# Weight low halves kept on chip between the two streams of a feed-forward up projection, and the inner products of that stage begun three pieces later

## The chip, the cores and the metric

The kernel runs on one core of a Trainium2 chip. The metric is the device time in microseconds (us) of one execution. A core has TensorE (matrix products, with weight loads beside them), VectorE, ScalarE, GpSimd, and SyncE, which here only issues loads. In profile lines they are PE (PEld for weight loads), DVE, ACT, POOL and SP.

## The reference

Two layers run over 256 latent tokens (`x`) and 256 context tokens (`xc`) of width 1024. Each layer has a mixer with three branches and then a convolutional feed-forward part; the change lies in the feed-forward part of the first layer, where both streams go through the same weights:

```python
def conv_ffn(h, w_up, conv_w, conv_b, w_down):
    u = h @ w_up                                  # (256, 1024) @ (1024, 5632)
    up = jnp.pad(u, ((0, 0), (1, 1), (0, 0)))
    u = up[:, :-2] * conv_w[0] + up[:, 1:-1] * conv_w[1] + up[:, 2:] * conv_w[2] + conv_b
    a, g = jnp.split(u, 2, axis=-1)
    return (a * jax.nn.silu(g)) @ w_down
...
    mod = (jax.nn.silu(c) @ w_mod[l] + b_mod[l])[:, None, :]
    mod_c = jax.nn.silu(c_ctx) @ w_mod[l] + b_mod[l]
    sh1, sc1, ga1, sh2, sc2, ga2 = jnp.split(mod, 6, axis=-1)
...
    x = x + ga1 * rms_norm(o, g_post_mix[l])
    f = conv_ffn(modulate(rms_norm(x, g_pre_ffn[l]), sh2, sc2), w_up[l], conv_w[l], conv_b[l], w_down[l])
    x = x + ga2 * rms_norm(f, g_post_ffn[l])
    if not last:
        ...
        xc = xc + cga1 * rms_norm(oc, g_post_mix[l])
        fc = conv_ffn(modulate(rms_norm(xc, g_pre_ffn[l]), csh2, csc2), w_up[l], conv_w[l], conv_b[l], w_down[l])
        xc = xc + cga2 * rms_norm(fc, g_post_ffn[l])
```

## The kernel before

**Split products.** Every float32 matrix is split into a high half (rounded to the matrix format, `hi`) and a low half (`lo`, the float32 value less `hi`). A product is three matrix products: high by high, high by low and low by high (`mm3`). The activations stand split in `HThi` and `HTlo`, 1024 channels by 512 tokens, of which columns 0 to 255 are the context and 256 to 511 the latent tokens.

**Pieces.** The whole kernel is a list `prog` of `Piece`s. A piece takes 512 KB of weights: here two blocks of 128 input channels by 512 output channels. Its weights are loaded to a `raw` buffer (five in all) by SyncE, ScalarE casts the high half (`split_hi`, L201), VectorE subtracts for the low half (`split_lo`, L205), and `emit` issues the products. A piece gives its raw buffer back at the end of `split_lo` (`use`), which lets the next load be issued. `run` goes through the list in order. Before it emits a piece it splits pieces ahead until two pieces that are still to come have been split. Pieces that hold no matrix product (the inner products below) do not count in these two, and are issued on VectorE as soon as the splitting reaches them. Instructions of one engine run in the order in which the program issues them. The tiles `whi` and `wlo` rotate through four buffers each.

**The up projection of the first layer.** `up(blk, (t0, t1))` appends the four pieces of block `blk` (256 value and 256 gate channels) for the tokens t0 to t1. The order is block 0 latent, block 1 latent, block 0 context, block 1 context, and then blocks 2 to 10 for both streams at once. So the weights of blocks 0 and 1 are loaded and split twice, in pieces `f0` to `f0 + 7` and again in `f0 + 8` to `f0 + 15`, because the context activations come later than the latent ones: the chain `c1c` (residual, normalisation, transposes, scaling, split) runs as side work, one step after each piece, and is finished before block 0 context. A 256-token piece is 24 products of 256 columns, a 512-token piece 24 of 512 columns. Two groups of 256 tokens share a PSUM bank. The two-group banks of blocks 0 and 1 and the four banks of block 2 come from the same four buffers, so that block 2 uses again the banks that the last 256-token blocks held. Odd blocks from 3 on use four others.

**Evacuation.** At the end of a block's last piece `ev_up` empties each group: ScalarE applies the middle convolution tap and the bias (L1356), VectorE adds the two neighbour taps (L1359; two large and two single-column instructions a group), later ScalarE applies silu (L1378, issued after the next piece), and GpSimd multiplies value by gate into `hT` (L1379).

**Inner products.** `mod_dot` computes modulation vectors (`ga2` of this layer, `sh1` and `sc1` of the next) on VectorE: for each 128 of 1024 outputs a 512 KB row block is loaded and multiplied with the condition vector of each stream, with accumulation (L451), so two instructions a piece. The 24 pieces are placed among the list's pieces by `spread(first, last, pieces)`, evenly from index `first` to `last`; here `first` is `f0 + 16`, the first piece of block 2.

**Slots.** `u()` hands out one of eight large slots, the longest free first, and `u_free` gives it back. In this stage the residual rows of both streams hold two, and each `hT` tile (four blocks of 128 channels) one, six at the end.

Of the kernel before, what the change touches and what calls it, by code (L numbers as in the profile page):

```python
# [9 lines left out]
F32R = mybir.dt.float32r  # L10
# [21 lines left out]
class Raw:  # L32
    def __init__(self, src, kk, n, early=False):
        self.early = early
        self.src, self.kk, self.n, self.tile, self.left = src, kk, n, None, 0


class Piece:
    def __init__(self, raw, emit, k0=0, kn=0, split=True, pre=None, side=1, need=None, share=None, dot=False):
        self.raw, self.emit, self.k0, self.kn, self.split = raw, emit, k0, kn, split  # L40
        self.pre, self.side, self.need = pre, side, need
        self.hi = self.lo = None
        self.dot = dot
        self.hold = self.fence = False
        self.share = share
        if raw:
            raw.left += 1


class Builder:  # L50
# [115 lines left out]
    def run(self):  # L166
        nc = self.nc
        prog = self.prog
        raws = []
        for p in prog:  # L170
            if p.raw and (not raws or raws[-1] is not p.raw):
                raws.append(p.raw)
        state = {"raw": 0, "live": 0, "split": 0}
        RB = 5

        def dma():
            while state["raw"] < len(raws):
                r = raws[state["raw"]]
                if r.early and self.free:
                    r.tile = self.u([128, r.kk, r.n], name="raw")  # L180
                elif state["live"] < RB:
                    r.early = False
                    r.tile = self.p_raw.tile([128, r.kk, r.n], F32, tag="raw", name="raw")
                    state["live"] += 1
                else:
                    break
                nc.sync.dma_start(out=r.tile, in_=r.src)
                state["raw"] += 1

        def use(p):  # L190
            p.raw.left -= 1
            if p.raw.left == 0:
                if p.raw.early:
                    self.u_free(p.raw.tile)
                else:
                    state["live"] -= 1
                dma()

        def split_hi(p):
            p.hi = self.p_w.tile([128, p.kn, p.raw.n], F32R, tag="hi", name="whi")  # L200
            nc.scalar.copy(p.hi, p.raw.tile[:, p.k0:p.k0 + p.kn, :])  # L201

        def split_lo(p):
            p.lo = self.p_w.tile([128, p.kn, p.raw.n], F32R, tag="lo", name="wlo")
            nc.vector.tensor_tensor(p.lo, p.raw.tile[:, p.k0:p.k0 + p.kn, :], p.hi.bitcast(F32), op=ALU.subtract)  # L205
            use(p)

        def split(p):
            if p.split:
                if p.hi is None:  # L210
                    split_hi(p)
                split_lo(p)

        def next_hi():
            q = prog[state["split"]]
            split_hi(q)
            return lambda: split_lo(q)
        self.next_hi = next_hi

        dma()  # L220
        ahead = 0
        for i, p in enumerate(prog):
            if i and prog[i].split and state["split"] > i:
                ahead -= 1
            if p.hold:
                p.need()
                if p.share:
                    state["split"] = i + 1
                split(prog[state["split"]])
                if state["split"] > i:  # L230
                    ahead += 1
                state["split"] += 1
                p.then()
            while state["split"] < len(prog) and state["split"] <= i + 6:
                q = prog[state["split"]]
                if q.hold and state["split"] > i or q.lo is None and state["split"] > i and prog[state["split"] - 1].fence:
                    break
                if state["split"] > i and q.split:
                    if ahead == 2:
                        break  # L240
                    ahead += 1
                if q.pre:
                    q.pre()
                if q.lo is None:
                    split(q)
                if q.dot:
                    q.emit(q.raw.tile)
                    use(q)
                state["split"] += 1
            if p.need and not p.hold:  # L250
                p.need()
            later, self.later = self.later, []
            if p.share:
                p.emit(p.share.hi, p.share.lo)
            elif p.split:
                p.emit(p.hi, p.lo)
            elif not p.dot:
                p.emit(p.raw.tile)
                use(p)
            for f in later:  # L260
                f()
            for _ in range(p.side):
                self.step()
# [851 lines left out]
    def layer(self, l):  # L1115
# [229 lines left out]
        def ev_up(blk):  # L1345
            def f(g, b):
                j, t0, t1 = g
                a = 2 * blk + j % 2
                ch = a if j < 2 else NFT + a
                n = t1 - t0  # L1350
                ta = self.t((128, n), name="ta")
                if L0:
                    tv, bv = self.halves(ta), self.unwoven(b[:, :n])
                else:
                    tv, bv = ta.unsqueeze(1), b[:, :n].unsqueeze(1)
                nc.scalar.activation(out=tv, in_=bv, func=ACTF.Identity, scale=cw[:, ch, 1:2], bias=cw[:, ch, 3:4])  # L1356

                def tap(o, x, t):
                    nc.vector.scalar_tensor_tensor(o, x, cw[:, ch, t:t + 1], o, op0=ALU.mult, op1=ALU.add)  # L1359

                def taps():
                    w = tv.shape[2]
                    tap(tv[:, :, 1:w], bv[:, :, 0:w - 1], 0)
                    tap(tv[:, :, 0:w - 1], bv[:, :, 1:w], 2)
                    if w == 128:
                        tap(tv[:, 1, 0:1], bv[:, 0, w - 1:w], 0)
                        tap(tv[:, 0, w - 1:w], bv[:, 1, 0:1], 2)
                    if j < 2:
                        st["ta", a] = ta
                        return  # L1370
                    if (l, "h", a // 4) not in st:
                        st[l, "h", a // 4] = self.u([128, 4, T], name="hT")
                    off = t0 - lat_all[0]
                    av = st.pop(("ta", a))
                    hv = st[l, "h", a // 4][:, a % 4, off:off + n]

                    def gate():
                        nc.scalar.activation(out=ta, in_=ta, func=ACTF.Silu)  # L1378
                        nc.gpsimd.tensor_tensor(hv, av, ta, op=ALU.mult)  # L1379
                    self.later.append(gate)  # L1380
                return taps
            return f
# [3 lines left out]
        def up(blk, r, **kw):  # L1386
            self.block(wu[:, :, blk, :], 8, 512, "wst", g4(r), X, ev_up(blk), main=4 if blk % 2 == 0 or (L0 and blk < 2) else 0,
                       pair=L0, **kw)
        f0 = len(self.prog)
        if L0:  # L1390
            up(0, (256, 512), need=lambda: self.finish("c1l"))
            up(1, (256, 512))
            up(0, (0, 256), need=lambda: self.finish("c1c"))
            up(1, (0, 256))
            for blk in range(2, 11):
                up(blk, (0, 512))
            self.spread(f0 + 16, len(self.prog), [p for l1, k in ((0, "ga2"), (1, "sh1"), (1, "sc1")) for p in self.mod_dot(l1, k)])
        else:
            for blk in range(11):
                up(blk, (256, 512))  # L1400
# [199 lines left out]
```

## Time and profile before

| | |
|---|---|
| median of 3 runs | 1506.92 us (1506.75 to 1507.0) |
| profiled execution | 1506.16 us, of which span 1504.4 us |
| granted TensorE clock, mean | 0.988 |
| TensorE, VectorE, ScalarE, GpSimd busy | 1442.5, 1073.0, 730.8, 212.4 us |
| low halves (L205) | 330 instructions, 413.3 us |
| inner products (L451) | 128 instructions, 157.4 us |
| first up projection of the first layer | about 580 to 826 us of the span |

The busy times are shares of one span and overlap. Products are pipelined: each is listed with its whole length, but the next begins before it ends. So the rate is read from the distance of the starts. In a timeline line stand the start, the length, the engine, the source line, the operation, the tiles written and read, the shape, the number of merged instructions, and in brackets the idle time before and what ended it. In a line of waits stand who waited for whom, the total, the count and the longest. In a table by windows stand, for each stretch, its length, and the busy time of each engine with its instruction count, the granted clock, the share of the DMA engines and GB/s. In the chain, a line is a start, a length and what ran.

### The profile page before, as it was taken

The numbers are of one execution on the slowest core, as the hardware profiler recorded it, in microseconds if no ns is written. First come the engines' busy times: TensorE is split into PE (matmuls) and PEld (weight loads), VectorE is DVE, ScalarE is ACT, GpSimd is POOL, SyncE is SP. The second block draws the span as 40 slices with busy tenths as digits, with TensorE's granted clock in tenths as the row PEclk, the third lists the DMA queues.
The fourth block names the chain that finished last, engine by engine and source line by source line (L and its number), as shares of the span: only waits on it lengthen the run. The fifth ranks groups of instructions, "written<-read, shape, count | busy, mean of one in ns | idle before, by whom it ended". The sixth has DMA issues, their size and how long they took to land.

```text
span 1504.4 us, 22921 instructions
## 1 busy us (share of the span) xinstructions
PE 1442.5 (96%) x8681; PEld 1251.2 (83%) x8681; DVE 1073.0 (71%) x1872; ACT 730.8 (49%) x1343; POOL 212.4 (14%) x312
## 2 busy tenths in 40 slices
PE   6999998999999999799999999999999899899997
PEld 3877786778888889788888888887978789799986
DVE  4438788776846578988887787738896556778874
ACT  3434443443455357433444566535544355566663
POOL 2000021002520121111111010100200330312100
PEclk9999999999999999999999999999999999999999
DMA  9623333333642356555454777634454545455662
GB/s 336 199 78 121 102 127 98 90 102 104 175 134 78 98 183 195 182 182 170 146 178 136 236 234 247 222 120 125 141 166 143 192 96 169 154 182 184 209 207 88
DMA packets 103806, 238.07 MB, mean 158 GB/s; under 512 B 8416, under 2 KB 18720, under 8 KB 103568
## 3 DMA queue, kind: packets, MB, share of 16 engines
q1 hardware_dynamic: 99472, 224.56, 46.8%
q0 software_dynamic: 4224, 12.05, 3.0%
q8 instruction: 68, 1.11, 0.3%
q14 instruction: 42, 0.34, 0.1%
HBM read 235.50 MB, written 1.08 MB: 157 GB/s over the span
## 4 chain that ended last, share of the span: by engine, by line
PE 82%; DVE 8%; ACT 3%; issue 3%; POOL 2%; DMA 1%; SPq 0%; DVEq 0%; POOLq 0%; ACTq 0%
PE bank L319 68%; PE bank L703 3%; PE bank L717 3%; PE bank L667 2%; PE bank L1028 2%; DVE wlo L205 2%; DVE ta L1359 1%; DVE jnk L451 1%; PE bank L421 1%; PE bank L664 1%; ACT whi L201 1%; PE bank L1005 1%; DMA raw<-in_w_mod 1%; DMA mb<-mrow 1%; POOL t L819 1%
## 5 line engine op out<-in xcount | busy, mean ns | idle before, releaser
L205 DVE TENSOR_TENSOR wlo<-raw,whi 128x1024 fp32r<-128x1024 f32 (+1 forms) x330 | 413.3, 1265 | 162.3 <-ACT whi L201 160.8
L319 PE MATMUL bank<-HThi,whi 128*128 128x256 f32 (+1 forms) x1408 | 464.5, 330 | 8.8 <-DVE ta L1359 4.5
L319 PE MATMUL bank<-HThi,wlo 128*128 128x256 f32 (+1 forms) x1408 | 459.9, 327 | 7.2 <-DVE wlo L205 7.0
L319 PE MATMUL bank<-HTlo,whi 128*128 128x256 f32 (+1 forms) x1408 | 459.6, 326 | 0.5 <-DVE HTlo L586 0.5
L201 ACT CAST whi<-raw 128x1024 fp32r<-128x1024 f32 (+1 forms) x330 | 335.8, 1037 | 175.1 <-PE bank L319 126.4
L319 PEld LDWEIGHTS bank<-HThi,whi 128*128 128x128 f32 x1408 | 270.2, 192 | 40.4 <-issue 15.5
L319 PEld LDWEIGHTS bank<-HThi,wlo 128*128 128x128 f32 x1408 | 270.2, 192 | 26.8 <-DVE wlo L205 8.7
L319 PEld LDWEIGHTS bank<-HTlo,whi 128*128 128x128 f32 x1408 | 270.5, 192 | 18.7 <-DVE HTlo L586 1.2
L319 PE MATMUL bank<-whi,xs 128*128 128x512 f32 x528 | 159.9, 381 | 0.9 <-DVE ta L1359 0.8
L451 DVE SCALAR_TENSOR_TENSOR jnk<-raw,CB 128x1024 bf16<-128x1024 f32 x128 | 157.4, 1229 | 1.8
L319 PE MATMUL bank<-whi,HThi 128*128 128x512 f32 (+1 forms) x384 | 142.5, 371 | 0.0
L1359 DVE SCALAR_TENSOR_TENSOR ta<-bank,cw,ta 128x255 f32<-128x255 f32 (+2 forms) x224 | 110.7, 527 | 41.7 <-ACT ta L1356 37.6
L319 PE MATMUL bank<-wlo,HThi 128*128 128x512 f32 (+1 forms) x384 | 139.1, 362 | 0.0
L319 PE MATMUL bank<-whi,HTlo 128*128 128x512 f32 (+1 forms) x384 | 139.1, 362 | 0.0
L319 PEld LDWEIGHTS bank<-whi,xs 128*128 128x128 f32 x528 | 99.8, 189 | 16.6 <-ACT ta L1378 1.3
L1356 ACT ACTIVATE ta<-bank,cw 128x256 f32<-128x256 f32 (+1 forms) x96 | 61.2, 646 | 101.9 <-PE bank L319 100.2
L679 ACT ACTIVATE pr<-bank,mn 128x512 f32<-128x512 f32 (+1 forms) x96 | 58.5, 614 | 89.0 <-DVE mn L676 80.6
L1379 POOL TENSOR_TENSOR hT<-ta 128x256 f32<-128x256 f32 (+1 forms) x48 | 56.6, 1182 | 309.3 <-ACT ta L1378 309.0
L319 PE MATMUL bank<-wlo,xs 128*128 128x512 f32 x264 | 100.1, 379 | 0.0
L319 PEld LDWEIGHTS bank<-whi,HThi 128*128 128x128 f32 x384 | 72.6, 189 | 20.4 <-issue 10.9
L319 PEld LDWEIGHTS bank<-whi,HTlo 128*128 128x128 f32 x384 | 72.6, 189 | 8.6
L319 PEld LDWEIGHTS bank<-wlo,HThi 128*128 128x128 f32 x384 | 72.6, 189 | 8.0
(228 smaller groups left out, 1728.9 us busy)
## 6 DMA issues: line engine op xcount, KB each, us to landing
raw<-in_w_in SPq DMA_DIRECT2D x112, 512.0 KB, 3.9
raw<-in_w_up SPq DMA_DIRECT2D x96, 512.0 KB, 4.6
raw<-in_w_modT SPq DMA_DIRECT2D x80, 512.0 KB, 4.2
raw<-in_w_down SPq DMA_DIRECT2D x66, 512.0 KB, 4.6
raw<-in_w_branch SPq DMA_DIRECT2D x24, 512.0 KB, 4.0
raw<-in_w_out SPq DMA_DIRECT2D x24, 512.0 KB, 4.2
raw<-in_w_mod SPq DMA_DIRECT2D x16, 512.0 KB, 10.5
nab<-in_nabias POOLq DMA_DIRECT2D x16, 256.0 KB, 4.1
```

The lines of the kernel that those rows point to most:

```text
L201: nc.scalar.copy(p.hi, p.raw.tile[:, p.k0:p.k0 + p.kn, :])
L205: nc.vector.tensor_tensor(p.lo, p.raw.tile[:, p.k0:p.k0 + p.kn, :], p.hi.bitcast(F32), op=ALU.subtract)
L319: nc.tensor.matmul(out, l, self.woven(r), start=first and i == 0, stop=last and i == 2)
L451: nc.vector.scalar_tensor_tensor(self.jnk, rt[:, 0, :], 1.0, self.CB[:, s, :], op0=ALU.mult, op1=ALU.mult, accum_out=dst[:, j, s:s + 1])
L667: nc.tensor.matmul(b, q[:, c0:c0 + 128], k[:, 0:512], start=True, stop=True)
L679: nc.scalar.activation(out=pt[:, w * i:w * i + w], in_=b[:, w * i:w * i + w], func=ACTF.Exp, scale=-1.0, bias=mn[:, i:i + 1], accum_out=mn ...
L703: nc.tensor.transpose(b[:, o:o + 128], pt[:, 128 * i:128 * i + 128], self.I)
L717: nc.tensor.matmul(b[64 * par:64 * par + 64, 0:w], v_of(p, par, kt), pTs[par][:, w * kt:w * kt + w], start=kt == 0, stop=kt == nkt - 1)
L1028: nc.tensor.matmul(b[:, d, 0:129], v[:, o:o + 128], V[:, s, h, :], start=n == 0, stop=n == len(sl) - 1)
L1356: nc.scalar.activation(out=tv, in_=bv, func=ACTF.Identity, scale=cw[:, ch, 1:2], bias=cw[:, ch, 3:4])
L1359: nc.vector.scalar_tensor_tensor(o, x, cw[:, ch, t:t + 1], o, op0=ALU.mult, op1=ALU.add)
L1379: nc.gpsimd.tensor_tensor(hv, av, ta, op=ALU.mult)
```

## The change

The low halves of pieces `f0` to `f0 + 7` are written to slots from `u()`, two pieces to a slot, four slots in all. Pieces `f0 + 8` to `f0 + 15` take these tiles as their low half and leave the subtraction out; they still load their weights and cast their high half. After the second piece of a pair has been emitted for the context, the slot is given back. The 24 inner-product pieces are spread from `f0 + 19` instead of `f0 + 16`.

```diff
         def split_lo(p):
-            p.lo = self.p_w.tile([128, p.kn, p.raw.n], F32R, tag="lo", name="wlo")
+            if p.lo_of:
+                p.lo = p.lo_of.lo
+                use(p)
+                return
+            p.lo = p.lo_at() if p.lo_at else self.p_w.tile([128, p.kn, p.raw.n], F32R, tag="lo", name="wlo")
             nc.vector.tensor_tensor(p.lo, p.raw.tile[:, p.k0:p.k0 + p.kn, :], p.hi.bitcast(F32), op=ALU.subtract)
             use(p)
...
             up(1, (256, 512))
             up(0, (0, 256), need=lambda: self.finish("c1c"))
             up(1, (0, 256))
+
+            kept = {}
+            for k in range(8):
+                p, q = self.prog[f0 + k], self.prog[f0 + 8 + k]
+
+                def put(k=k):
+                    if k % 2 == 0:
+                        kept[k // 2] = self.u([128, 2, 2, 512], F32R, name="keep")
+                    return kept[k // 2][:, k % 2]
+
+                def done(hi, lo, k=k, emit=q.emit):
+                    emit(hi, lo)
+                    if k % 2:
+                        self.u_free(kept[k // 2])
+                p.lo_at, q.lo_of, q.emit = put, p, done
             for blk in range(2, 11):
                 up(blk, (0, 512))
-            self.spread(f0 + 16, len(self.prog), [p for l1, k in ((0, "ga2"), (1, "sh1"), (1, "sc1")) for p in self.mod_dot(l1, k)])
+            self.spread(f0 + 19, len(self.prog), [p for l1, k in ((0, "ga2"), (1, "sh1"), (1, "sc1")) for p in self.mod_dot(l1, k)])
```

More of the change, by code (lines that the diff above doesn't have):

```diff
@@ L42, in __init__ @@
         self.hi = self.lo = None
+        self.lo_at = self.lo_of = None
         self.dot = dot
```

## Prediction

> **What bounds the kernel now.** I read the page first (shares, then the chain that ended last), then TensorE's waits in the stage that is edited, then the order of time on TensorE, VectorE and ScalarE there, and last the stretch behind it.
>
> ```profile
> PE 1442.5 (96%) x8681; PEld 1251.2 (83%) x8681; DVE 1073.0 (71%) x1872; ACT 730.8 (49%) x1343; POOL 212.4 (14%) x312
> ...
> PE 82%; DVE 8%; ACT 3%; issue 3%; POOL 2%; DMA 1%; SPq 0%; DVEq 0%; POOLq 0%; ACTq 0%
> ...
> PE bank L319 <- DVE wlo L205: 4.6, 4, 1.8
> PE bank L319 <- DVE ta L1359: 4.5, 2, 3.5
> ...
> core 0: us, PE busy (x) PEld busy (x) DVE busy (x) ACT busy (x) POOL busy (x), PEclk, DMA share, GB/s
> 604.77:639.39 34.62, 27.10 (x218) 25.41 (x216) 31.37 (x67) 15.33 (x26) 4.49 (x5) 1.00 0.59 194
> 640.00:660.70 20.70, 20.70 (x98) 18.12 (x97) 18.90 (x25) 9.55 (x12) 2.45 (x3) 1.00 0.56 178
> 764.30:785.00 20.70, 20.70 (x98) 18.12 (x97) 19.05 (x25) 9.08 (x12) 2.57 (x3) 1.00 0.54 178
> ...
> 639.84 166.19 PE bank L319 x770
> ```
>
> Over the whole span TensorE is busy 96% and carries 82% of the chain: only places where it stands still can give time. The waits are those of 602 to 640 us: six, four on the subtraction that makes a low half (L205), two on the convolution taps (L1359). In the third group, 604.77 to 639.39 is the context half of blocks 0 and 1: VectorE is busy 31.37 of 34.62 us, TensorE 27.10, so VectorE sets the pace. Behind it the chain is one piece, 770 products in 166.19 us (0.2158 us each): TensorE never waits there, so what the earlier stage gains is passed on whole.
>
> I number the weight pieces of the up projection 0 to 15: 0-3 and 4-7 are blocks 0 and 1 for the latent rows, 8-11 and 12-15 the same for the context rows; piece 16 is the first of block 2. A piece is 24 products.
>
> ```profile
> 602.78 0.38 PE L319 MATMUL bank<-HThi,wlo 128*128 128x256 f32 x1 [1.57 <-DVE wlo L205]
> 603.00 0.28 PE L319 MATMUL bank<-HThi,whi 128*128 128x256 f32 x1
> ...
> 603.89 0.28 PE L319 MATMUL bank<-HThi,wlo 128*128 128x256 f32 x1
> ...
> 606.05 0.38 PE L319 MATMUL bank<-HThi,wlo 128*128 128x256 f32 x1 [0.32 <-DVE wlo L205]
> 613.46 0.38 PE L319 MATMUL bank<-HThi,wlo 128*128 128x256 f32 x1 [1.78 <-DVE wlo L205]
> 625.37 0.38 PE L319 MATMUL bank<-HThi,wlo 128*128 128x256 f32 x1 [0.92 <-DVE wlo L205]
> 636.81 0.45 PE L319 MATMUL bank<-HThi,whi 128*128 128x512 f32 x1 [3.46 <-DVE ta L1359]
> 639.39 0.45 PE L319 MATMUL bank<-HThi,whi 128*128 128x512 f32 x1 [1.04 <-DVE ta L1359]
> ```
>
> From 603.00 to 603.89 are eight steps of 0.111 us, so an unhindered piece takes 24 x 0.11125 = 2.67 us. The waits end at the third product of pieces 7, 8, 10 and 14 (the first that needs a low half), and at groups 2 and 3 of piece 16, whose PSUM banks the taps of piece 15 must have read. From 602.78 to 639.39 (36.61 us) TensorE does 22 + 8 x 24 = 214 short products (23.81 us) and 18 long ones (3.88 us): 8.9 us are lost. Split by the same count (24, 48, 96, then 46 + 12 long, then 6 long products between the rows) this is 0.6 before piece 8, 2.1 before piece 10, 1.2 before piece 14, 3.7 and 1.3 at piece 16.
>
> **The change part by part.** The order on VectorE is that of the program:
>
> ```profile
> 604.16 0.69 DVE L586 TENSOR_TENSOR HTlo<-ht,HThi 128x512 fp32r<-128x512 f32 x1
> 604.77 2.35 DVE L205 TENSOR_TENSOR wlo<-raw,whi 128x1024 fp32r<-128x1024 f32 x2
> 607.04 5.22 DVE L1359 SCALAR_TENSOR_TENSOR ta<-bank,cw,ta 128x254 f32<-128x254 f32 x16
> 612.19 1.21 DVE L205 TENSOR_TENSOR wlo<-raw,whi 128x1024 fp32r<-128x1024 f32 x1
> 613.75 3.60 DVE L205 TENSOR_TENSOR wlo<-raw,whi 128x1024 fp32r<-128x1024 f32 x3 [0.35 <-ACT whi L201]
> 618.73 5.45 DVE L1359 SCALAR_TENSOR_TENSOR ta<-bank,cw,ta 128x254 f32<-128x254 f32 x16 [1.37 <-ACT ta L1356]
> 624.09 1.22 DVE L205 TENSOR_TENSOR wlo<-raw,whi 128x1024 fp32r<-128x1024 f32 x1
> 625.65 1.34 DVE L205 TENSOR_TENSOR wlo<-raw,whi 128x1024 fp32r<-128x1024 f32 x1 [0.34 <-ACT whi L201]
> 626.92 1.21 DVE L451 SCALAR_TENSOR_TENSOR jnk<-raw,CB 128x1024 bf16<-128x1024 f32 x1
> ...
> 629.33 2.36 DVE L205 TENSOR_TENSOR wlo<-raw,whi 128x1024 fp32r<-128x1024 f32 x2
> ...
> 634.01 5.23 DVE L1359 SCALAR_TENSOR_TENSOR ta<-bank,cw,ta 128x254 f32<-128x254 f32 x16
> ```
>
> Behind the last low half of the context activations (L586) these are the low halves of pieces 8, 9; taps of 7; low halves of 10; 11, 12, 13; taps of 11; low halves of 14 and 15; a first inner-product piece (two passes over a row of 1024, one per stream, 626.92 to 629.33, 2.4 us); low halves of 16, 17; a second inner-product piece (to 634.01); taps of 15. The change takes out the eight subtractions of pieces 8 to 15 (some 1.2 us each) and puts both inner-product pieces behind the taps of 15, since the first now stands in front of piece 19 and the loop prepares only two pieces ahead.
>
> The casts of the high halves stay. ScalarE's rows give the two delays that the new order keeps:
>
> ```profile
> 604.23 1.06 ACT L1356 ACTIVATE ta<-bank,cw 128x256 f32<-128x256 f32 x2
> 612.68 2.93 ACT L201 CAST whi<-raw 128x1024 fp32r<-128x1024 f32 x3
> 617.62 1.02 ACT L1356 ACTIVATE ta<-bank,cw 128x256 f32<-128x256 f32 x2 [2.00 <-PE bank L319]
> 624.59 2.93 ACT L201 CAST whi<-raw 128x1024 fp32r<-128x1024 f32 x3
> 629.47 1.02 ACT L1356 ACTIVATE ta<-bank,cw 128x256 f32<-128x256 f32 x2 [1.95 <-PE bank L319]
> ```
>
> Taps start 1.11 us after ScalarE's first evacuation where VectorE is free (617.62 to 618.73). ScalarE starts 0.3 to 0.4 us after the twelfth product of a block's last piece (617.62 against 613.46 + 34 x 0.11125 = 617.24; 629.47 against 629.15). Three casts follow 5.86 us after a start of taps (618.73 to 624.59), behind the gates of that block.
>
> The new course, from 602.78, up to which nothing changes:
> - Piece 8 starts 22 products later, at 605.23, and has its low half. The last write of its context activations (604.16, 0.69 us) ends by 604.9, in time.
> - Taps of 7 start at 604.23 + 1.11 = 605.34 instead of 607.04; casts of 11 to 13 at about 611.0 instead of 612.68, done for 11 by 612.0, and piece 11 begins at 605.23 + 3 x 2.67 = 613.24.
> - Taps of 11: twelfth product 614.58, ScalarE 614.95, VectorE 616.06. Casts of 15, 16, 17 at 621.9 to 624.9; piece 15 begins at 623.92, its cast is done at 622.9. Low halves of 16 and 17 end by 626.25.
> - Taps of 15: twelfth product 625.26, ScalarE 625.57, VectorE 626.68. In the old run group 2 of piece 16 started 2.80 us and group 3 5.38 us after these taps began (634.01 to 636.81 and 639.39). So group 2 may start at 629.48 where TensorE is ready at 626.59 + 12 x 0.2158 = 629.18 (0.3 lost), and group 3 at 632.06 where it is ready at 630.78 (1.3 lost).
>
> Group 3 of piece 16 then starts at 632.06 instead of 639.39: **7.3 us less** (8.9 lost before, 1.6 left). What is late next is the chain from the last product of piece 15 through ScalarE and the taps to the bank. In parts: with the products left where they are, they would push the taps of 15 to about 628.6 and the gain would be 5.4; with the products moved alone, ScalarE's 629.47 would let the taps start at 630.6 and the gain would be 3.4.
>
> Parts that I cost at nothing, and their bounds:
> - The moved products (24 pieces over 33 body pieces instead of 36) fall into the stretch where TensorE never waits. A block there takes 20.7 us; blocks with three of them now keep VectorE busy 18.90 and 19.05, and 24 over 33 is 2.9 per block. Cover 1.6 us a block. Without cover the two early ones would cost 2 x 2.4 = 4.8.
> - Low halves of 0 to 7 go to another buffer with the same shape, by the same instruction: 0 by the row of 1.22, up to 0.1 each by the slowest row (1.34), of which only piece 7's lies on the path.
> - SyncE's loads keep their number. A raw buffer of pieces 8 to 15 is given back by ScalarE's cast instead of the subtraction, so loads go out earlier; each inner-product load goes out three pieces later, behind the loads of 16 to 18, and is needed only by VectorE. Piece 17's load goes out after cast 12 (612.9) and lands 4.5 us later by the row below, against its cast at 623.9. A piece in 2.67 us asks 196 GB/s; the stage already moved 194 with the DMA engines 0.59 busy.
> - Four slots are held for the kept halves, beside two of residual rows and one of gated outputs: seven of eight. The context rows' load gets another slot, whose last readers, the merged branch products, ended by 541 (L1204 below, last start 539.3); the load stays where it is, at 565.14.
>
> ```profile
> raw<-in_w_up SPq DMA_DIRECT2D x25, 512.0 KB, 4.5
> ...
> 658.82 3.56 POOL L1379 TENSOR_TENSOR hT<-ta 128x512 f32<-128x512 f32 x2 [18.25 <-ACT ta L1378]
> ...
> 659.19 4.27 DVE L205 TENSOR_TENSOR wlo<-raw,whi 128x1024 fp32r<-128x1024 f32 x2
> ...
> L1204 DVE SCALAR_TENSOR_TENSOR HTlo<-sig,HThi x8: 677/680/1766, 526.0 to 539.3; 128x512 fp32r<-128x512 f32 x8
> ...
> 565.14 0.79 POOL L642 DMA_DIRECT2D x<-in_ctx  x1
> ...
> 598.84 0.97 DVE L585 CAST HThi<-ht 128x512 fp32r<-128x512 f32 x1 [0.62 <-ACT ht L582]
> ...
> 598.00 0.36 PE L319 MATMUL bank<-HThi,whi 128*128 128x256 f32 x1
> ```
>
> **The rivals.**
> 1. Slower: VectorE becomes the bound of blocks 2 to 10. Beside GpSimd's two gated products (658.82) a pair of subtractions took 4.27 us where the pair of 629.33 took 2.36: 1.9 us. Inner products also read two operands, and more of them now follow each block's taps. Three a block come to 4 x 1.2 + 3 x 2.4 + 5.9 = 17.9 us without such a loss; two losses make 21.7, 1.0 over the 20.7, and eight blocks would give 8.0 back: 1507.6. It decides from 3.7 us of loss a block. Against it: the blocks that have three read 18.90 and 19.05, losses included, with TensorE unbroken.
> [...]
> 2. Pieces share a kept tile in pairs. If products waited for the whole tile, piece 6 would wait for the low half of 7 (its third product at 602.78 instead of some 598.3; one piece, 2.67 us, lost) and piece 2 some 1.1 us for that of 3: gain 3.5, 1503.4. Against it: at 598.84 VectorE writes the context half of HThi while TensorE, from 598.00, reads the latent half with no wait, so halves of a tile are kept apart.
> 3. The change does half of what it says: the products still come up ahead of the taps of 15. Gain 5.4: 1501.5. Against it: the order above is just what the two-piece look-ahead gives.
>
> **How the numbers follow.** The profiled execution took 1506.16 us (span 1504.4, 1.8 around it), 0.8 below the median of the runs, 1506.92; the difference is taken from the median: 1506.92 - 7.3 = 1499.6. Chances: the forecast 0.80 (its own range 1498.6 to 1500.6, VectorE ready for the taps of 15 0.4 us early, or 1 us late); rival 2 0.06; rival 3 0.04; rival 1 0.07, of which 0.04 at the full price or more and 0.03 where it eats most of the gain; 0.03 for a gain of 8 to 9 (all 8.9 us). A measurement of this kernel tells about 0.2% (3.0 us) from no change. Faster: 0.80 + 0.06 + 0.04 + 0.03, less 0.02 for rival 2 with a small gain, 0.91; same 0.05; slower 0.04. The range runs from 1498.0 (all of 8.9) to 1502.0 (rival 3, and the bound of the slower subtractions).
>
> **What would show it.** Right: ten subtractions between 604.77 and the second block's start become two; no wait on L205 in pieces 8 to 15; taps of 7, 11 and 15 start near 605.3, 616.1 and 626.7; the first inner-product pass after the taps of 15; one or two short waits on L1359 at piece 16, together 1.6 us; then one unbroken piece of some 166 us or more on TensorE. Wrong: a wait on L205 in pieces 2, 4 or 6 (rival 2), an inner product ahead of the taps of 15 (rival 3), waits on L1359 or L205 between 640 and 800 (rival 1), or the casts of the high halves becoming what pieces 11 or 15 wait for.

## The result, and the profile after

The changed kernel takes 1498.34 us in the median (1495.86 to 1500.67), against 1506.96 before (1506.75 to 1507.04): ratio 0.9941, 95% interval 0.9929 to 0.9953, so 7.1 to 10.7 us less. Forecast were 1499.6 in a range of 1498.0 to 1502.0. The profiled execution took 1497.82 us, its span 1496.0 against 1504.4.

The lines of the file have moved by five: the subtraction is L210, the products L324, the taps L1364, the inner products L456. First TensorE's waits from 605 to 640 us, then windows of the stage and of two blocks behind it (columns as before), then the long piece of the chain:

```profile
PE bank L324 <- DVE ta L1364: 1.0, 1, 1.0
...
605.06:632.37 27.31, 26.27 (x218) 25.18 (x216) 17.46 (x52) 16.27 (x27) 3.71 (x5) 1.00 0.62 207
633.00:653.70 20.70, 20.70 (x98) 18.12 (x97) 18.60 (x25) 8.70 (x11) 2.86 (x3) 1.00 0.53 178
715.80:736.50 20.70, 20.70 (x98) 18.12 (x97) 17.75 (x24) 8.24 (x11) 2.56 (x3) 1.00 0.55 178
...
632.37 178.96 PE bank L324 x828
```

Of the five waits in pieces 8 to 16 one is left, the last, at a bank of piece 16. VectorE is busy 17.46 of 27.31 us where it was 31.37 of 34.62: it no longer sets the pace, and TensorE is busy 26.27. Behind the stage the chain is one piece again. VectorE's order of time in the new stage, and TensorE's starts of piece 0, of piece 7 behind its wait, and of groups 0, 2 and 3 of piece 16:

```profile
605.62 5.25 DVE L1364 SCALAR_TENSOR_TENSOR ta<-bank,cw,ta 128x254 f32<-128x254 f32 x16 [0.47 <-ACT ta L1361]
616.38 5.24 DVE L1364 SCALAR_TENSOR_TENSOR ta<-bank,cw,ta 128x254 f32<-128x254 f32 x16 [5.52 <-ACT ta L1361]
624.05 2.36 DVE L210 TENSOR_TENSOR wlo<-raw,whi 128x1024 fp32r<-128x1024 f32 x2 [2.43 <-ACT whi L202]
626.99 5.24 DVE L1364 SCALAR_TENSOR_TENSOR ta<-bank,cw,ta 128x254 f32<-128x254 f32 x16 [0.57 <-ACT ta L1361]
632.14 1.21 DVE L210 TENSOR_TENSOR wlo<-raw,whi 128x1024 fp32r<-128x1024 f32 x1
633.27 1.77 DVE L456 SCALAR_TENSOR_TENSOR jnk<-raw,CB 128x1024 bf16<-128x1024 f32 x1
...
580.44 0.38 PE L324 MATMUL bank<-HThi,whi 128*128 128x256 f32 x1 [0.62 <-DVE o L623]
603.07 0.38 PE L324 MATMUL bank<-HThi,keep 128*128 128x256 f32 x1 [1.56 <-DVE keep L210]
627.07 0.38 PE L324 MATMUL bank<-HThi,whi 128*128 128x512 f32 x1
...
629.80 0.45 PE L324 MATMUL bank<-HThi,whi 128*128 128x512 f32 x1
632.37 0.45 PE L324 MATMUL bank<-HThi,whi 128*128 128x512 f32 x1 [1.04 <-DVE ta L1364]
```

Ten subtractions have become two, all three groups of taps now wait for ScalarE (0.47, 5.52 and 0.57 us), where before only those of piece 11 did, and the first inner product comes after the taps of piece 15. Piece 0 before:

```profile
580.15 0.38 PE L319 MATMUL bank<-HThi,whi 128*128 128x256 f32 x1 [0.61 <-DVE o L618]
```

It now starts 0.29 us later (580.44), so group 3 of piece 16 comes 51.93 us after it where it came 59.24: **7.31 us less in the stage**.

The span of the profiled execution fell by 8.4 us, though. Two marks further on place the rest: the gate-row transposes of the first down projection, and the first 512-column product of layer 2. Before, then after:

```profile
870.09 1.04 PE L606 MATMUL bank<-ident,ga 128*128 128x128 f32 x8
968.37 0.48 PE L319 MATMUL bank<-HThi,whi 128*128 128x512 f32 x1 [0.37 <-DVE HThi L585]
```

```profile
863.03 1.04 PE L611 MATMUL bank<-ident,ga 128*128 128x128 f32 x8
959.79 0.48 PE L324 MATMUL bank<-HThi,whi 128*128 128x512 f32 x1 [0.48 <-DVE HThi L590]
```

Between the marks lie 98.28 us before and 96.76 after: 1.5 us in a stretch that no edit touches. What differs there is the granted clock, the column ahead of the DMA share. Both executions wait 1.82 us for the same low half; before, then after:

```profile
959.22 0.38 PE L319 MATMUL bank<-HThi,wlo 128*128 128x256 f32 x1 [1.82 <-DVE wlo L205]
...
961.00:963.00 2.00, 2.00 (x12) 2.00 (x11) 2.00 (x4) 0.04 (x1) 0.00 (x0) 0.52 1.02 353
```

```profile
952.16 0.38 PE L324 MATMUL bank<-HThi,wlo 128*128 128x256 f32 x1 [1.82 <-DVE wlo L210]
...
954.00:956.00 2.00, 2.00 (x20) 2.00 (x20) 2.00 (x4) 0.06 (x1) 0.00 (x0) 1.00 1.00 362
```

In the one the clock fell to 0.50 behind the wait, from 959.50 to 962.91, 12 products in 2 us instead of 20; in the other it did not. The experiments had two questions: whether the stage's gain is made of the parts as the prediction put them, and whether the 1.3 us by which the median gained more (8.6 against 7.3) come from this clock.

### The profile page after: what moved, and what is told of

Its sections match the earlier page's. It is cut to its first block, busy times and chain, and to the rows that moved or that the text cites. A ratio compares the mean times of both kernels' runs of the same rounds, so it can differ in the third digit from the quotient of the medians.

```text
span 1496.0 us, 22913 instructions
## 1 busy us (share of the span) xinstructions
PE 1439.7 (96%) x8681; PEld 1249.1 (83%) x8681; DVE 1061.6 (71%) x1864; ACT 731.0 (49%) x1343; POOL 212.1 (14%) x312
## 3 DMA queue, kind: packets, MB, share of 16 engines
q8 instruction: 68, 1.11, 0.3%
## 4 chain that ended last, share of the span: by engine, by line
PE 84%; DVE 7%; ACT 3%; issue 2%; POOL 2%; DMA 2%; SPq 0%; DVEq 0%; POOLq 0%; ACTq 0%
PE bank L324 70%; PE bank L708 3%; PE bank L722 3%; PE bank L672 2%; PE bank L1033 2%; DVE wlo L210 1%; DVE ta L1364 1%; DVE jnk L456 1%; DMA mb<-mrow 1%; ACT whi L202 1%; PE bank L669 1%; PE bank L426 1%; PE bank L1010 1%; DMA raw<-in_w_mod 1%; POOL t L824 1%
## 5 line engine op out<-in xcount | busy, mean ns | idle before, releaser
L210 DVE TENSOR_TENSOR wlo<-raw,whi 128x1024 fp32r<-128x1024 f32 (+1 forms) x314 | 390.9, 1257 | 166.6 <-ACT whi L202 165.2
L324 PE MATMUL bank<-HThi,whi 128*128 128x256 f32 (+1 forms) x1408 | 463.2, 329 | 5.4 <-DVE HThi L590 3.1
L324 PE MATMUL bank<-HTlo,whi 128*128 128x256 f32 (+1 forms) x1408 | 458.8, 326 | 0.5 <-DVE HTlo L591 0.5
L324 PE MATMUL bank<-HThi,wlo 128*128 128x512 f32 (+1 forms) x1280 | 423.5, 331 | 2.6 <-DVE wlo L210 2.6
L324 PEld LDWEIGHTS bank<-HThi,whi 128*128 128x128 f32 x1408 | 269.3, 191 | 36.9 <-issue 12.0
L324 PEld LDWEIGHTS bank<-HTlo,whi 128*128 128x128 f32 x1408 | 269.4, 191 | 18.8 <-DVE HTlo L591 1.1
L324 PEld LDWEIGHTS bank<-HThi,wlo 128*128 128x128 f32 x1280 | 244.8, 191 | 21.3 <-DVE wlo L210 3.3
L324 PE MATMUL bank<-whi,xs 128*128 128x512 f32 x528 | 159.9, 381 | 0.9 <-DVE ta L1364 0.8
L456 DVE SCALAR_TENSOR_TENSOR jnk<-raw,CB 128x1024 bf16<-128x1024 f32 x128 | 158.1, 1235 | 1.8
L324 PE MATMUL bank<-whi,HThi 128*128 128x512 f32 (+1 forms) x384 | 142.5, 371 | 0.0
L1364 DVE SCALAR_TENSOR_TENSOR ta<-bank,cw,ta 128x255 f32<-128x255 f32 (+2 forms) x224 | 110.7, 527 | 42.5 <-ACT ta L1361 38.5
L324 PE MATMUL bank<-wlo,HThi 128*128 128x512 f32 (+1 forms) x384 | 139.1, 362 | 0.0
L324 PE MATMUL bank<-whi,HTlo 128*128 128x512 f32 (+1 forms) x384 | 139.1, 362 | 0.0
L324 PEld LDWEIGHTS bank<-whi,xs 128*128 128x128 f32 x528 | 99.8, 189 | 16.6 <-ACT ta L1383 1.3
L324 PE MATMUL bank<-wlo,xs 128*128 128x512 f32 x264 | 100.1, 379 | 0.0
L324 PEld LDWEIGHTS bank<-whi,HThi 128*128 128x128 f32 x384 | 72.6, 189 | 20.4 <-issue 10.8
L324 PEld LDWEIGHTS bank<-whi,HTlo 128*128 128x128 f32 x384 | 72.6, 189 | 8.6
L324 PEld LDWEIGHTS bank<-wlo,HThi 128*128 128x128 f32 x384 | 72.6, 189 | 8.0
```

The lines of the kernel that those rows point to most:

```text
L324: nc.tensor.matmul(out, l, self.woven(r), start=first and i == 0, stop=last and i == 2)
L456: nc.vector.scalar_tensor_tensor(self.jnk, rt[:, 0, :], 1.0, self.CB[:, s, :], op0=ALU.mult, op1=ALU.mult, accum_out=dst[:, j, s:s + 1])
```

## The experiments

All times of piece 16 and of the gate rows below are from the first product of piece 0, worked out from the starts in the trace of each run. The medians come from three series, each with the kernel before run beside it: 1506.96 us beside the first of the changed kernel, 1508.14 beside its six further runs and the next three rows, 1507.87 beside the last row. So a median is compared with the one beside it.

| kernel | to group 3 of piece 16 | to the gate rows | median us |
|---|---|---|---|
| before | 59.24 | 289.94 | 1506.96 |
| before, two more profiles | 59.25, 59.37 | 290.40, 291.61 | 1506.37, 1507.84 (one run each) |
| changed | 51.93 | 282.59 | 1498.34 |
| changed, three more profiles | 51.93, 51.93, 51.94 | 282.60 each | 1498.53 (six runs); 1497.70, 1496.86 (one run each) |
| kept halves alone | 54.00 | 287.30 | 1501.35 |
| later products alone | 55.76 | 286.47 | 1502.34 |
| changed, banks exchanged | 50.51 | 281.10 | 1496.99 |
| before, filled at piece 16 | 59.24 | 289.95 | 1505.44 |

**The kept halves alone.**

```diff
-            self.spread(f0 + 19, len(self.prog), ...
+            self.spread(f0 + 16, len(self.prog), ...
```

> Only the kept low halves; the inner products stay spread from the first piece of block 2. Theory A (VectorE's order sets the stage): the taps of piece 15 start near 628.6 us, two inner-product pieces ahead of them, and group 3 of piece 16 starts near 634.0 instead of 639.4, 5.4 us less than before. Rival (the products' place carries the gain): under 1 us less at that point. Theory B (clock) says that the total can lie up to some 2.5 us to either side of what this stage gives, with the spread between runs, and that the stage's own number has no such spread.

VectorE's taps of 15, TensorE at piece 16, and a window behind it:

```profile
627.11 5.22 DVE L1364 SCALAR_TENSOR_TENSOR ta<-bank,cw,ta 128x254 f32<-128x254 f32 x16
...
629.91 0.45 PE L324 MATMUL bank<-HThi,whi 128*128 128x512 f32 x1 [2.03 <-DVE ta L1364]
...
632.48 0.77 PE L324 MATMUL bank<-HThi,whi 128*128 128x512 f32 x1 [0.75 <-DVE ta L1364]
...
633.00:636.00 3.00, 3.00 (x8) 2.35 (x7) 2.19 (x2) 2.74 (x3) 0.66 (x1) 0.50 0.02 5
...
632.48 181.61 PE bank L324 x828
```

Piece 0 starts at 578.48 here, so the taps of 15 stand at 628.8 on the scale of before (forecast 628.6), and group 3 comes 5.24 us earlier (forecast 5.4). Behind the wait of 2.03 us the clock fell to 0.50: the same 828 products took 181.61 us instead of 178.96, and half of the gain was gone by the gate rows (2.64 us left). The run's time: ratio 0.9957, interval 0.9946 to 0.9969.

**The later products alone.** Only the spread from `f0 + 19`, on the kernel before.

> Only the later inner products; all low halves are subtracted twice as before. Theory A: ScalarE's evacuation at 629.5 lets the taps of piece 15 start at 630.6, group 3 of piece 16 starts near 636.0, 3.4 us less than before; the waits on the subtractions of pieces 8, 10 and 14 stay (0.6, 2.1, 1.2 us lost). Rival (the products' place carries the gain): 7 us less. The sum of both parts alone, 8.8, is more than the 7.3 of both together, since each also shortens the wait before the taps of 15.

```profile
PE bank L319 <- DVE wlo L205: 3.0, 3, 1.8
PE bank L319 <- DVE ta L1359: 1.0, 1, 1.0
...
630.65 5.23 DVE L1359 SCALAR_TENSOR_TENSOR ta<-bank,cw,ta 128x254 f32<-128x254 f32 x16 [1.25 <-ACT ta L1356]
...
636.03 0.46 PE L319 MATMUL bank<-HThi,whi 128*128 128x512 f32 x1 [1.04 <-DVE ta L1359]
```

The three waits on low halves stay, the long wait at piece 16 goes; piece 0 starts at 580.27 here, so the taps of 15 stand at 630.53 on the scale of before (forecast 630.6), and group 3 comes 3.48 us earlier (forecast 3.4). Neither part carries the gain alone: 5.24 and 3.48 make 8.7, both together 7.31, as worked out ahead. The ratio of the run, 0.9961, interval 0.9950 to 0.9973, is not told apart from the kept halves alone.

**The changed kernel once more.**

> The changed kernel once more, for its spread. Theory B (the granted clock falls for some 3.4 us after a short idle stretch of TensorE in some executions and not in others): times between 1495.5 and 1501, and the lower the mean granted clock, the longer the span; group 3 of piece 16 again 7.3 us earlier than before against the stage's start. Rival (the spread was chance of one chip): all runs within 0.5 us.

The six runs lie between 1496.74 and 1503.44, one of them above the range expected, and the stage takes 51.93 us again. The kernel before, run beside it, spread from 1506.32 to 1509.73, so its four close times in the first comparison do not show its spread. Over the six runs the changed kernel's span fell as the mean granted clock rose, from 1501.7 us at 0.985 to 1495.0 at 0.989.

**Exchanged banks.**

```diff
-            self.block(..., main=4 if blk % 2 == 0 or (L0 and blk < 2) else 0,
+            self.block(..., main=4 if blk % 2 == L0 or (L0 and blk < 2) else 0,
```

> The changed kernel with the PSUM banks of blocks 2 to 10 of the first layer exchanged (even blocks in the second set of four), so that piece 16 needs no bank of block 1 and the down projection none of block 10. Theory A: the last wait at piece 16 (1.6 us lost) goes, and the one at the first product of the down projection (0.6 idle, some 0.8 lost) too: 2.4 us less than the changed kernel, by the order of the stage. Rival (the wait on VectorE only moves, to the low half of 17 or 18): 0 to 0.5 us less.

TensorE at the start of the down projection, VectorE ahead of it (L1431 makes the low half of the gated rows) and the next two VectorE rows, and GpSimd beside them:

```profile
814.97 2.71 POOL L1384 TENSOR_TENSOR hT<-ta 128x512 f32<-128x512 f32 x2 [18.39 <-ACT ta L1383]
815.10 1.43 DVE L1431 TENSOR_TENSOR xs<-hT,xs 128x256 fp32r<-128x256 f32 x1
...
816.46 2.31 DVE L210 TENSOR_TENSOR wlo<-raw,whi 128x1024 fp32r<-128x1024 f32 x1
...
818.68 0.41 DVE L1431 TENSOR_TENSOR xs<-hT,xs 128x256 fp32r<-128x256 f32 x1
819.02 1.21 DVE L210 TENSOR_TENSOR wlo<-raw,whi 128x1024 fp32r<-128x1024 f32 x1
...
818.82 0.48 PE L324 MATMUL bank<-wlo,xs 128*128 128x512 f32 x1 [1.11 <-DVE wlo L210]
```

The wait at piece 16 is gone (1.42 us). The one at the down projection is only replaced: free of its bank, TensorE now waits 1.11 us for the low half of 816.46, queued behind the taps of block 10. That subtraction and the instruction ahead of it took 2.31 and 1.43 us, where the next of each kind, with GpSimd done, took 1.21 and 0.41. These 2.1 us are more than the wait, so VectorE rows this much slower beside GpSimd, the loss that rival 1 names, are enough to account for it; no run leaves them out. At the gate rows 1.5 us are gained instead of 2.4.

**Filled waits.** Products of no use on TensorE in two stretches of layer 2 where it stands idle, on the kernel before, on the changed one, and on the one with exchanged banks:

```diff
+    def fill(self, n, c0):
+        spare = self.bank(False)
+        for i in range(n):
+            self.nc.tensor.matmul(spare[:, 0:256], self.HThi[:, 0, c0:c0 + 128], self.HThi[:, 1, c0:c0 + 256], start=i == 0, stop=i == n - 1)
...
-        for _ in range(1 + wait):
+        for i in range(1 + wait):
             yield
+            if wait == 3 and s == CTXS and i == 1:
+                self.fill(16, 256)
...
+            self.fill(36, 0)
             turned = [self.tile_turn(xns[1], 1, h) for h in range(2)]
```

> The kernel before, with products of no use on TensorE in two stretches where it stands idle: 16 of 256 columns (1.8 us) ahead of the piece of layer 2's first projection that waits 1.8 us for a low half (at 959 in the run before), and 36 (4.0 us) ahead of the transposes in layer 2's feed-forward start that wait 4.8 us. Theory B: the granted clock stays at 1.00 in 950 to 970 and in 1305 to 1325, where it stood at 0.5 for some 3.4 us; each such stretch costs 1.6 us, so 1.6 to 3.2 us less than before. Rival (the low clock is not set off by the idle time but comes at its own times): no change in the clock there, and 0 to 0.5 us more than before.

> The changed kernel with the same two fillings. Theory B: clock 1.00 at the same two places, 1.6 to 2.5 us less than the changed kernel, and its difference from the kernel before with the fillings comes to the 7.3 us of the stage, give or take 1.5 us for the low-clock stretches that remain near 240, 1160 and 1220. Rival: the difference stays near 9 us, so that the change gains outside its stage by something other than the clock.

> The changed kernel with exchanged banks and both fillings: the parts add up, 2.4 us for the banks and 1.6 to 2.5 us for the clock, 1494 us. Rival: the fillings take PSUM banks that the exchanged blocks need, and a wait on the taps or on a filling appears at the start of layer 2's up projection; then no gain over the exchanged banks alone.

The second stretch before, then filled (kernel before), then filled (changed kernel):

```profile
1315.00:1318.00 3.00, 2.36 (x10) 1.88 (x10) 2.30 (x9) 2.02 (x6) 0.00 (x0) 0.50 0.34 130
```

```profile
1315.00:1318.00 3.00, 1.95 (x15) 1.68 (x15) 2.76 (x9) 3.00 (x9) 0.00 (x0) 1.00 0.05 20
```

```profile
1308.00:1311.00 3.00, 3.00 (x18) 3.00 (x17) 2.86 (x5) 2.89 (x4) 0.00 (x0) 0.56 0.00 0
```

The kernel before went from 1507.60 to 1503.89 (ratio 0.9977, 0.9967 to 0.9987), 3.7 us where 1.6 to 3.2 were expected, and spread over 1.9 us only; the changed one went to 1495.96 (0.9924, 0.9910 to 0.9938). Their difference is 7.9 us, nearer to the stage's 7.3 than the 9.6 us of the unfilled pair that ran together (1508.14 and 1498.53); but the interval of that pair's ratio, 0.9927 to 0.9954, is 6.9 to 11.0 us, so the times alone do not tell the two differences apart. In the profiles the first stretch ran at 1.00 in all three filled kernels, where the clock had fallen in five of eleven profiles without the filling. The second ran at 1.00 in two of the three, where it stood at 0.50 in the first profile of before, in the first of its two further ones and in the first of the changed kernel; in the filled changed kernel the clock fell there all the same, to 0.56. So in these profiles the fall was rarer with the stretches filled, and not excluded. With exchanged banks as well the time is 1495.91 (0.9919, 0.9906 to 0.9932) where 1494 was expected: the fastest here with the filled changed kernel, and not told apart from it. The rival's wait on the taps or on a filling does not appear; the 1.5 us of the banks do not show above the spread.

**More profiles of both.**

> The kernel before once more, for one profile. Theory B (the 1.2 us by which the median gained more than the stage come from the granted clock at the start of layer 2): the clock stands near 0.5 for some 3.4 us behind the wait of 1.8 us near 959, and from the gate-row transposes of the first down projection to the first 512-column product of layer 2 pass 98.3 us. Rival (it is the landing of loads there): this stretch varies by 1 to 2 us with the clock at 1.00.

> As the other look at the kernel before: 98.3 us with the low clock by theory B; 59.2 us from piece 0 to group 3 of piece 16.

> The changed kernel once more, for one profile. Theory B: no low clock behind the same wait near 952, and 96.8 us for the same stretch. Rival: a stretch of 98 us with the clock at 1.00. Both: from the first product of piece 0 to group 3 of piece 16 again 51.9 us.

> As the other look at the changed kernel: 96.8 us without the low clock by theory B; 51.9 us from piece 0 to group 3 of piece 16.

From the gate rows to the first 512-column product of layer 2 the four, two of before and two of the changed kernel, passed 96.64, 96.76, 96.68 and 97.02 us, all with the clock at 1.00. Over all profiles this stretch is 98.3 us with the low clock (before, both single parts, exchanged banks, and the last kernel below) and 96.6 to 97.0 without. But theory B's forecast for before failed: the clock did not fall there in either. It fell at another place instead, at the wait of 3.5 us at piece 16. The second of the two:

```profile
637.38 0.76 PE L319 MATMUL bank<-HThi,whi 128*128 128x512 f32 x1 [3.45 <-DVE ta L1359]
...
637.40:640.40 3.00, 3.00 (x7) 2.27 (x8) 2.26 (x8) 0.92 (x3) 0.75 (x2) 0.50 0.27 108
640.40:643.40 3.00, 3.00 (x8) 2.35 (x8) 2.12 (x2) 2.74 (x3) 0.73 (x1) 0.52 0.03 5
```

Part of that is hidden under the wait of group 3, the rest is lost: 0.5 and 1.7 us by the gate rows (290.40 and 291.61 against 289.94). In the changed kernel all four profiles stand at 1.00 there.

**Piece 16 filled, in the kernel before.** `self.fill(28, 256)` ahead of the products of piece 16, nothing else.

> The kernel before with 28 products of no use (256 columns, 3.1 us) ahead of piece 16, in the time in which TensorE waits there for the taps of piece 15. Theory B (that wait of 3.5 us lets the clock fall, in three of four profiles of before and its filled version, and costs 0.1 to 1.7 us behind it): clock 1.00 from 635 to 645, 289.9 us from the first product of piece 0 to the gate-row transposes of the first down projection, and up to 0.6 us less than before in the median, which may not show above the spread. Rival: the low clock comes there all the same, or the fill delays piece 16 and costs 0.5 us or more.

```profile
638.73 0.45 PE L319 MATMUL bank<-HThi,whi 128*128 128x512 f32 x1 [1.03 <-DVE ta L1365]
...
638.00:641.00 3.00, 2.27 (x11) 2.03 (x12) 1.48 (x4) 2.32 (x4) 1.36 (x2) 1.00 0.00 0
...
869.44 1.04 PE L612 MATMUL bank<-ident,ga 128*128 128x128 f32 x8
```

Piece 0 starts at 579.49 here. Group 3 and the gate rows come as in the first profile of before (59.24, 289.95), with the clock at 1.00, and the median is 1505.44 against 1507.87 beside it: ratio 0.9986, interval 0.9975 to 0.9998. By this interval twenty-eight products that compute nothing save 0.3 to 3.8 us, just clear of no change. The middle of it, 2.4 us in the medians, is more than the 0.6 expected at most; how much of it belongs to piece 16 and how much is chance at the other places, this interval does not settle.

## Why the prediction was right, point by point

- *VectorE's order sets the stage.* Shown. On the scale of before (0.29 us taken off) the taps of 7, 11 and 15 started at 605.33, 616.09 and 626.70; forecast were 605.34, 616.06 and 626.68. Group 3 of piece 16 came at 632.08, forecast 632.06. Piece 16 began at 626.78 (forecast 626.59), and the two losses behind that were 0.14 and 1.28 (forecast 0.3 and 1.3). Each part alone gave its own forecast within 0.2 us.
- *What is late next.* Right: the only wait left in pieces 8 to 16 is on the taps of 15, and exchanging the banks took it away.
- *Moved products cost nothing.* Right: in eight stretches of 20.7 us from 633 on VectorE is busy 15.4 to 18.6 us, and TensorE does not wait between 632.4 and 811. Rival 1 falls for these blocks; the loss that it names is there. The first inner-product pass (from 633.27) took 1.77 us instead of 1.22, right where GpSimd multiplies (a product of 1.15 us from 632.81). The cover took the loss.
- *Rival 2* falls: piece 6 did not wait for its neighbour's half, the wait stays at piece 7 (603.07). *Rival 3* falls by the order above.
- *The size.* 8.6 us came in the median where 7.3 were forecast. The forecast lies inside the measured 7.1 to 10.7, so the times alone do not show that more was gained. What the sum "8.9 us are lost" left at nothing is the clock: it priced each wait by its own length, in one execution in which the clock had stayed at 1.00 at piece 16. In two further profiles of before it fell there, which adds 0.5 and 1.7 us that the change takes away with the wait; in all four profiles of the changed kernel it stayed up there. In the profiled pair another 1.5 us lie in the clock at the start of layer 2. It fell there in one of three profiles of before, in none of four of the changed kernel, and in that kernel with exchanged banks, so this part of the 8.4 us is not shown to belong to the change and is best called luck. The split of the 1.3 us between these places is not shown.
- *The clock.* In the first profile of before it stands at 0.50 for 3.41 us from 959.50 and from 1229.15, and for 6.83 us from 246.11, 1171.12 and 1314.48. The length of a wait alone does not decide here whether it falls. The wait of 1.81 or 1.82 us at the start of layer 2 was followed by the fall in five of the eleven profiles in which it was not filled, and the one of 2.03 us at piece 16, with the kept halves alone, was too. The wait of before at piece 16 was followed by it in both further profiles (3.45 us each) and not in the first (3.46 us). Three rows of the first profile, the second of them at that wait:

```profile
246.11:252.94 6.83, 5.82 (x17) 3.61 (x18) 3.53 (x10) 2.58 (x8) 0.00 (x0) 0.50 0.00 2
637.00:640.00 3.00, 1.96 (x9) 1.42 (x9) 2.10 (x8) 1.08 (x3) 0.89 (x2) 1.00 0.15 59
959.50:962.91 3.41, 3.41 (x18) 3.41 (x18) 3.41 (x5) 0.00 (x0) 0.00 (x0) 0.50 0.79 233
```

What decides it from one execution to the next is not shown.

## What to carry to other kernels

Where an engine that isn't the busiest over the whole kernel is full in one stage, write its instructions down in program order, strike what the edit takes out, and carry the starts forward with the delays that the old trace shows: this gave group 3 of piece 16 to 0.02 us. Work that has no date belongs behind the instructions that free a bank or a buffer, and two parts that shorten the same wait gain less together (7.31 us) than the sum of what each gains alone (8.7). Behind waits of TensorE of 1.81 to 3.45 us the clock fell in some executions here and not in others, and the low clock cost up to 2.6 us again; so price such a wait with a margin above. Where it can't be removed, a few products of no use in it can be worth more than they cost: two waits filled gave the kernel before 3.7 us.

## What was not expected of the hardware

- The clock fell to half behind a wait of 2.03 us with 2.65 us of loss over the next 828 products, and behind waits of 1.81 or 1.82 us in five of the eleven profiles in which the start of layer 2 was not filled. Series of five runs or more of a kernel with no filling spread over 3.1 to 6.7 us. In most of them the longer spans have the lower mean granted clock, but not in all: among twelve runs of the kernel before, a span of 1504.7 us has 0.985 and one of 1504.2 has 0.988.
- Taking a wait away can move it by one instruction only: with the banks exchanged, a wait on a bank became one of 1.11 us on a low half in the same place, where two VectorE instructions beside GpSimd took 2.1 us longer than their next of kind.
